# A hybrid decoder step on one core: the memory's statistics, the order of the key projections and the even mixer's PSUM tiles

## The chip, the cores and the metric

The kernel runs on one NeuronCore of a Trainium2 chip, as one launch. The metric is the device time of that launch in microseconds (us); a lower time is better. Five engines take part: TensorE (PE, matmuls; its weight loads are listed as PEld), VectorE (DVE), ScalarE (ACT), GpSimd (POOL) and SyncE (SP), which issues most of the DMAs. Each engine works through its own list of instructions in the order in which they were written, and waits where an operand or a buffer isn't ready.

## The reference

It is one inference step of a decoder with two layers, for 256 prompt tokens and 8 x 8 sample tokens that share all weights. The kernel handles them as 320 columns. All is float32, the model width is 2048.

```
layer i:  x += Mixer_i(rmsnorm(x))            # i = 0: even mixer, i = 1: odd mixer
          x += MemCrossAttn(rmsnorm(x), mem)
          x += SqReLU_MLP(rmsnorm(x))
even:     [silu(layernorm(dwconv(glu(h W)))), dilated attention(h W)] W_out
def mem_kv(mem, g_mem, wk, wv, kn):           # mem: 256 rows of 2048, the same in both layers
    m = rmsnorm(mem, g_mem)
    k = rmsnorm((m @ wk) as 4 heads of 128, kn)
    v = (m @ wv) as 4 heads of 128
```

The prompt's queries attend over these keys and values; the sample tokens attend over given caches. The keys and values of both layers are outputs too. The mean square of a memory row depends on the memory alone, so one value serves K and V of both layers, and since it scales a whole row, it can be applied to the projected row.

## The kernel before

**Weights.** All weight matrices are streamed in a fixed order as 800 "halves" of 128 x 1024 float32 (512 KB, tile `raw`, issued by SP, four buffers). Each half is split into two fp32r parts: ACT makes `whi` (L152), DVE makes the rest `wlo` (L153), three halves before PE uses them. An activation is split in the same way into `h` and `l`, and each product is three matmuls: whi by h, whi by l, wlo by h (L220 to L222). A half is 24 matmuls of 320 columns.

**Lanes.** Everything that isn't a product of the stream runs in Python generators ("lanes"). `pump()` and `mini()` advance each of them by a step after a half or half of one, and the instructions are emitted at that place. So the order on every engine is written out by the program; a scheduler doesn't change it. A `yield` in a lane moves what follows it to the next step.

**Around the change.** The stages are: the even mixer (input projection, convolution, attention), its output projection (even_out, eight residual steps p = 0 to 7), memory attention of layer 0 (K0, q, V0, K1, wo: K1 is the key projection of layer 1), FFN 0, the odd mixer, memory attention of layer 1 (q, V1, wo), FFN 1.

- `memkv(l, part)` makes a projection of the memory. Its `prep(k)` splits one of 16 blocks of 128 x 256: hi on ACT (L274), lo on DVE (L275), from a piece `z` of the memory (256 KB; 8 pieces). For K0 (`sums=True`), ACT also squares each piece (L303) and POOL adds the squares up (L304). `ahead(n)` prepares the first n blocks; in `body` five blocks are prepared before PE uses the first (L344 to L346 for keys, 256 columns; L352 to L354 for values, 512 columns).
- `statistics()` sums the squares over the partitions with a matmul by ones (L320) and makes the reciprocal root (`newton`) in `mrow` and `rcol`. It runs in the lane "fin" after K0, ahead of the keys' own norm: `finish()` squares the scaled keys and sums them by a matmul (L388, two instructions for each of two halves p).
- In even_out's residual step, DVE adds the product to `x` (L900), ACT makes the next activation's high parts and a square (L884, L889), DVE the low parts and the running sum of squares (L893, L896). K0's first pieces are loaded at p = 4, and its first three blocks prepared at p = 6 (L988 and after).
- After the last step, POOL sums the squares of `x` across the partitions (`across`, L253), and ACT and DVE make `rr`.
- In the even mixer, PSUM has, beside the two tiles of the main products, one tile of two banks (`pn`) and two single banks (`pa`). Scores (L779, L781), turned probabilities, weights per head (L706) and the convolution's layer norm take tiles from them; a new tile waits until the reader of the old one is done.

Of the kernel before, what the change touches and what calls it, by code (L numbers as in the profile page):

```python
# [20 lines left out]
P = 128  # L21
T = 320
# [86 lines left out]
def program(nc, tc, i, o):  # L109
# [12 lines left out]
    pn = es.enter_context(tc.tile_pool(name="pn", bufs=1, space=PSUM))  # L122
    pa = es.enter_context(tc.tile_pool(name="pa", bufs=2, space=PSUM))
# [157 lines left out]
    def memkv(l, part, new, sums=False, follow=None, deep=3):  # L281


        piece, hl, acc = {}, {}, []

        def load(q):
# [3 lines left out]
            elif follow:  # L290
                follow[0](q - 8)

        def prep(k):
# [22 lines left out]

        def statistics():
            V.tensor_add(out=acc[0][:, 0, :], in0=acc[0][:, 0, :], in1=acc[0][:, 1, :])
            ps = mk(pa, [P, 512], "a")
            mm(out=ps[:, :TP], lhsT=ones, rhs=acc[0][:, 0, :], start=True, stop=True)  # L320
            s, r = new("mrs", [P, TP], F32), new("mr", [P, TP], F32)
            newton(ps[:, :TP], D, s, r)
            V.tensor_mul(out=r, in0=r, in1=s)
            mrow.append(r)

            t = acc[0].rearrange("p a (b c) -> p (a b) c", c=P)[:, :2, :]
            V.tensor_mul(out=t, in0=r.rearrange("p (b c) -> p b c", c=P), in1=bc(ident, 2))
            V.tensor_reduce(out=rcol, in_=t, axis=AX.X, op=ALU.add)

        def body():  # L330
# [36 lines left out]
            if part == "K" and not sums:  # L367
# [7 lines left out]
            def finish():  # L375
                while l and (lanes.get("pr") or lanes.get("sa")):
                    yield
                if sums:
                    yield
                    statistics()  # L380
                    scaled()
                for p, z in enumerate(zs):
# [3 lines left out]
                    yield from pause(1 + l)  # L386
# [10 lines left out]
        return start, ahead, body, load  # L397
# [4 lines left out]
    with tc.tile_pool(name="even", bufs=1) as ep:  # L402
# [133 lines left out]
        def conv_ln():  # L536
            yield from pause(4)
            ps = mk(pn, [P, 2, 512], "n")
            for e in range(2):
                mm(out=ps[:, 0, :T], lhsT=ones, rhs=ysum[:, e, :], start=(e == 0), stop=(e == 1))  # L540
            mean = mk(ep, [P, T], "odd")
            nc.scalar.mul(out=mean, in_=ps[:, 0, :T], mul=1.0 / 1024)
# [10 lines left out]
            ps = mk(pn, [P, 2, 512], "n")  # L553
            for e in range(2):
                mm(out=ps[:, 0, :T], lhsT=ones, rhs=ysum[:, e, :], start=(e == 0), stop=(e == 1))
            s, r = mk(ep, [P, T], "cbuf", bufs=2), mk(ep, [P, T], "odd")
            newton(ps[:, 0, :T], 1024, s, r)
# [44 lines left out]
        def values(vs, pr, g):  # L602
# [6 lines left out]
            n = mk(pn, [P, 2, 512], "n")  # L609
            for e in range(4):  # L610
                nc.tensor.transpose(n[:, 0, e * P:e * P + P], vs[:, e // 2, (e % 2) * P:(e % 2) * P + P], ident)
            vt = mk(ep, [P, 4, P], f"vtok{g}")
            nc.scalar.copy(out=vt.rearrange("p a b -> p (a b)"), in_=n[:, 0, :])
            vtok[pr, g] = vt
            if g == 2:
                yield
                yield
                n = mk(pn, [P, 2, 512], "n")
                for s in range(4):
                    nc.tensor.transpose(n[:96, 0, s * P:s * P + P], vcat[pr][:, s, :], ident)  # L620
                vn = mk(ep, [P, 4, P], "vnew")
                nc.scalar.copy(out=vn[:96].rearrange("p a b -> p (a b)"), in_=n[:96, 0, :])
# [147 lines left out]
        def prompt(pr):  # L770
# [3 lines left out]
            for h in range(2):  # L774
                qk_ = [(qk[pr, 0, g][:, h, :], qk[pr, 1, g][:, h, :]) for g in range(3)]
                Sp = mk(ep, [P, 1152], "Sp")
                ps, n = mk(pa, [P, 512], "a"), mk(pn, [P, 2, 512], "n")
                for g, (q, k) in enumerate(qk_):
                    mm(out=ps[:, g * P:g * P + P], lhsT=q[:, :P], rhs=k[:, :P], start=True, stop=True)  # L779
                for g, (q, k) in enumerate(qk_):  # L780
                    mm(out=n[:, g // 2, g % 2 * TP:g % 2 * TP + TP], lhsT=q[:, P:TP], rhs=k[:, :TP], start=True, stop=True)  # L781
# [14 lines left out]
                ps, n = mk(pa, [P, 512], "a"), mk(pn, [P, 2, 512], "n")  # L796
                for g, dst in enumerate((ps, n[:, 0, :], n[:, 1, :])):
# [3 lines left out]
                nc.scalar.copy(out=pt[:, 0, :], in_=ps[:, :384])  # L801
                nc.scalar.copy(out=pt[:, 1:3, :], in_=n[:, :, :384])
# [68 lines left out]

    xp = es.enter_context(tc.tile_pool(name="xp", bufs=1))
# [63 lines left out]
    def memattn(l, before):  # L936

        with tc.tile_pool(name=f"mem{l}", bufs=1) as mp:
            KV = 3
            kvt = {}  # L940
            turn = {"first": itertools.cycle(("Xh6", "Xl6", "Xl7", "Xh0", "Xl0", "Xh1", "Xl1")), "mhl": itertools.cycle([f"Y{c}{n}" for n in range(4) for c in "hl"]), "mf": itertools.cycle(("Xl6", "Xl7")),
                    "mraw": itertools.cycle(("xacc", "xsq", "xsq"))}

            def room0(name, shape, dt):
                if name == "mhl":
                    return mk(base, shape, next(turn["first"]), dt, 1)
                if name in ("macc", "msq"):
                    return mk(base, shape, {"macc": "Xh7", "msq": "Xl5"}[name], dt, 1)
                if name == "mraw":
                    return mk(xp, shape, "z", dt, 2)  # L950
                if name in ("mk0", "mk1"):
                    return mkt[:, 2 * int(name[2]):2 * int(name[2]) + 2, :].rearrange("p a b -> p (a b)")
                return room(name, shape, dt)

            def room(name, shape, dt):
                if name in ("mf0", "mf1", "mf2"):
                    return mk(base, shape, next(turn["mf"]), dt, 1)
                if name == "mhl":
                    return mk(xp, shape, next(turn["mhl"]), dt, 1)
                if name in ("mv0", "mv1"):  # L960
                    return mvt[:, int(name[2]), :]
                if name == "mraw":
                    t = next(turn[name])
                    return mk(xp, shape, t, dt, {"xacc": 1, "xsq": 2}[t])
                if name in ("mrs", "mr"):
                    return mk(*((xp, [P, T], "rs") if name == "mrs" else (mp, shape, "mr")), dt)[:, :TP]
                return mk(xp, shape, "z", dt, 2)

            mstart, mahead, mbody, mload = memkv(1, "KV"[l], room)
            nstart, nahead, nbody, _ = memkv(0, "V", room, follow=(mload, mahead)) if l == 0 else (mstart, mahead, None, None)  # L970
# [71 lines left out]
            def prompt():  # L1042
# [39 lines left out]
                yield from pause(2 - l)  # L1082
                for p in range(2):
# [8 lines left out]
                    if l == 0:  # L1092
                        yield

            def sample():
                for p in range(2):
                    while p not in ready:
                        yield
                    yield from pause(5 - 3 * l * p)
# [21 lines left out]
                    while l and p and not have:  # L1121
# [19 lines left out]
            gemm(src, evac(0), after=lambda q: nstart() if q == 3 else None)  # L1141
            gemm(src, evac(1), after=lambda q: nahead(6) if q == 2 else None)
            if nbody:
                nbody()
                have.append(1)
            mbody()
# [367 lines left out]
```

## Time and profile before

| | us |
|---|---|
| median of 3 runs | 2978.48 (2975.43 to 2978.82) |
| the profiled execution | 2979.26 |
| its span, first to last instruction | 2977.5 |
| PE busy | 2936.9 (99%) |
| DVE busy | 1660.1 (56%) |
| ACT busy | 1195.6 (40%) |
| POOL busy | 133.8 (4%) |
| DMA, mean over the span | 170 GB/s |
| TensorE's mean granted clock | 0.995 |

The chain that ended last runs over PE for 95% of the span. An idle time of PE is therefore time of the kernel; an idle time of another engine matters where PE waits for it. All times in the rows are microseconds from the start of the span, unless a row says ns. The names of tiles are the program's, without buffer numbers.

### The profile page before, as it was taken

To read this page: it belongs to the slowest core of one execution; us is meant where nothing else is said; L and a number is where in the kernel's file an instruction comes from. 1 tells how busy PE (TensorE), PEld (TensorE's weight loads), DVE (VectorE), ACT (ScalarE), POOL (GpSimd) and SP (SyncE) were. 2 spreads that over 40 slices of the span, in tenths; PEclk is the share of its full clock that TensorE was granted. 3 is DMA by queue.
4 is the path that set the end of the run, shared out by engine and by line. 5 is a ranking of instruction groups with operands and counts; after the bars stand their busy time and mean duration, and the time that the engine had idled before them with its cause. 6 is when DMAs were issued, how large, how long until landed. Compare 5 with 4: busy or idle time off the path is not lost.

```text
span 2977.5 us, 49080 instructions
## 1 busy us (share of the span) xinstructions
PE 2936.9 (99%) x20828; PEld 2893.5 (97%) x20828; DVE 1660.1 (56%) x1903; ACT 1195.6 (40%) x1493; POOL 133.8 (4%) x115
## 2 busy tenths in 40 slices
PE   8999989899999999999999999999999999999999
PEld 8999989789999999999999999999999999999999
DVE  7887965577544544544545467557544544544543
ACT  6544454465333333333334344446332332332332
POOL 2210310200000000000000000000000000000000
PEclk9999999899999999999999999999999999999999
DMA  6774676464444444444444444555444444444443
GB/s 244 278 273 140 220 252 224 156 252 158 151 149 148 150 150 148 154 150 142 156 149 161 151 150 147 195 181 199 152 149 149 150 152 152 149 149 149 150 157 126
DMA packets 142253, 506.84 MB, mean 170 GB/s; under 512 B 16209, under 2 KB 18769, under 8 KB 139985
## 3 DMA queue, kind: packets, MB, share of 16 engines
q1 hardware_dynamic: 139536, 495.77, 47.5%
q0 software_dynamic: 2496, 7.92, 0.7%
q8 instruction: 163, 2.67, 0.4%
q14 instruction: 58, 0.47, 0.0%
HBM read 493.09 MB, written 10.54 MB: 169 GB/s over the span
## 4 chain that ended last, share of the span: by engine, by line
PE 95%; DVE 2%; ACT 1%; issue 1%; DMA 0%; POOL 0%; SPq 0%; DVEq 0%; POOLq 0%; ACTq 0%
PE g L220 30%; PE g L222 30%; PE g L221 29%; DVE wlo L153 1%; PE g L352 1%; PE g L354 0%; PE g L353 0%; PE a L689 0%; PE g L345 0%; PE a L718 0%; PE g L346 0%; PE g L344 0%; ACT whi L152 0%; DMA raw<-in_wall 0%; PE n L1297 0%
## 5 line engine op out<-in xcount | busy, mean ns | idle before, releaser
L153 DVE TENSOR_TENSOR wlo<-raw,whi 128x1024 fp32r<-128x1024 f32 x800 | 994.8, 1252 | 916.0 <-ACT whi L152 898.8
L152 ACT CAST whi<-raw 128x1024 fp32r<-128x1024 f32 x800 | 835.9, 1049 | 1119.9 <-PE g L221 1069.4
L220 PE MATMUL g<-Xh,whi 128*128 128x320 f32 x3424 | 1061.5, 310 | 8.7 <-ACT whi L152 8.4
L222 PE MATMUL g<-Xh,wlo 128*128 128x320 f32 x3424 | 1055.5, 308 | 0.4 <-DVE wlo L153 0.4
L221 PE MATMUL g<-Xl,whi 128*128 128x320 f32 x3424 | 1055.6, 308 | 0.0
L220 PE MATMUL g<-Yh,whi 128*128 128x320 f32 x2688 | 834.0, 310 | 2.2 <-DVE x L900 2.2
L222 PE MATMUL g<-Yh,wlo 128*128 128x320 f32 x2688 | 831.3, 309 | 0.0
L221 PE MATMUL g<-Yl,whi 128*128 128x320 f32 x2688 | 831.2, 309 | 0.0
L220 PEld LDWEIGHTS g<-Xh,whi 128*128 128x128 f32 x3424 | 643.8, 188 | 14.7 <-ACT whi L152 9.0
L221 PEld LDWEIGHTS g<-Xl,whi 128*128 128x128 f32 x3424 | 643.8, 188 | 0.5 <-issue 0.2
L222 PEld LDWEIGHTS g<-Xh,wlo 128*128 128x128 f32 x3424 | 643.5, 188 | 0.8 <-DVE wlo L153 0.8
L220 PEld LDWEIGHTS g<-Yh,whi 128*128 128x128 f32 x2688 | 505.3, 188 | 4.0 <-issue 3.5
L221 PEld LDWEIGHTS g<-Yl,whi 128*128 128x128 f32 x2688 | 505.2, 188 | 0.7 <-issue 0.5
L222 PEld LDWEIGHTS g<-Yh,wlo 128*128 128x128 f32 x2688 | 505.2, 188 | 0.0
L270 ACT CAST Xh<-z 128x640 fp32r<-128x640 f32 x72 | 52.3, 727 | 300.8 <-DVE z L1188 273.7
L1187 DVE TENSOR_TENSOR z<-g,rr 128x640 f32<-128x640 f32 x64 | 52.8, 825 | 82.5 <-PE g L222 82.5
L271 DVE TENSOR_TENSOR Xl<-z,Xh 128x640 fp32r<-128x640 f32 x72 | 59.5, 826 | 57.1 <-ACT Xh L270 57.1
L1203 DVE TENSOR_TENSOR x<-x,g 128x640 f32<-128x640 f32 x48 | 39.4, 821 | 64.9 <-PE g L222 64.9
L524 DVE SCALAR_TENSOR_TENSOR y<-cbuf,cst,y 128x320 f32<-128x320 f32 x120 | 68.5, 570 | 2.7 <-ACT y L522 2.7
L900 DVE TENSOR_TENSOR x<-x,g 128x640 f32<-128x640 f32 x48 | 39.4, 821 | 53.8 <-PE g L222 52.8
L253 POOL PARTITION_ALL_REDUCE xacc<-xacc x7 | 19.6, 2796 | 1102.7 <-DVE xacc L921 956.7
L524 DVE SCALAR_TENSOR_TENSOR odd<-cbuf,cst,odd 128x320 f32<-128x320 f32 x112 | 61.4, 548 | 0.0
(337 smaller groups left out, 1477.5 us busy)
## 6 DMA issues: line engine op xcount, KB each, us to landing
raw<-in_wall SPq DMA_DIRECT2D x800, 512.0 KB, 3.3
kv<-in_kv SPq DMA_DIRECT2D x72, 512.0 KB, 6.5
kv<-in_memc SPq DMA_DIRECT2D x16, 1024.0 KB, 6.9
xsq<-in_mem SPq DMA_DIRECT2D x15, 256.0 KB, 4.2
x<-in_x SPq DMA_DIRECT2D x8, 320.0 KB, 5.2
out_y<-x SPq DMA_DIRECT2D x8, 320.0 KB, 2.3
xacc<-in_mem SPq DMA_DIRECT2D x9, 256.0 KB, 3.6
z<-in_mem SPq DMA_DIRECT2D x8, 256.0 KB, 2.8
```

What stands on the lines that cost most here:

```text
L152: nc.scalar.copy(out=hi, in_=src)
L153: V.tensor_sub(out=lo, in0=src, in1=hi.bitcast(F32))
L220: mm(out=out, lhsT=w1, rhs=ah, start=(k == 0), stop=False)
L221: mm(out=out, lhsT=w1, rhs=al, start=False, stop=False)
L222: mm(out=out, lhsT=w2, rhs=ah, start=False, stop=(k == nk - 1))
L270: nc.scalar.copy(out=hi, in_=src)
L271: V.tensor_sub(out=lo, in0=src, in1=hi.bitcast(F32))
L352: mm(out=out, lhsT=m1, rhs=w1, start=(k == 0), stop=False)
L524: V.scalar_tensor_tensor(out=out, in0=buf[:, :, j:j + 8], scalar=w, in1=out, op0=ALU.mult, op1=ALU.add)
L900: V.tensor_add(out=x[p], in0=x[p], in1=ps[:, :, :T])
L1187: V.tensor_mul(out=z, in0=ps[:, :, :T], in1=bc(r.r, 2))
L1203: V.tensor_add(out=x[p], in0=x[p], in1=ps[:, :, :T])
```

## The change

- **Statistics.** They leave `memkv` and become a generator `memstat` in a lane "stat", which runs beside even_out. It loads the eight pieces of the memory once more, squares each in its own buffer on ACT, adds on DVE (not POOL), and ends with the matmul by ones and `newton`.
- **Order of the stream in layer 0.** It was K0, q, V0, K1; now it is K0, K1, q, V0. K1's body follows K0's directly and has blocks of its own (eight tiles; K0 has seven). K0 starts K1's loads and first blocks.
- **K0's start.** Its first two loads are issued at p = 6 (before at p = 4), and its first three blocks are prepared at p = 7 (before at p = 6). Both keys are scaled by `mrow` at the end of their body.
- **Lanes of layer 0.** `finish` has one `yield` and waits for nothing else. The prompt and sample lanes have the pauses that layer 1 had.
- **PSUM of the even mixer.** A pool `pe` of four single banks takes the place of `pn` and `pa`, which are opened after the even mixer. The scores' mask is added in three pieces (384, 512 and 256 columns; before 384 and 768), and the turned probabilities are copied in three pieces of 384 columns (before 384 and 768).

```
             memkv(0, "K")
+            memkv(1, "K")
         pairs("wq_mem", l, list(range(16)), 2)
-        if l == 0:
-            memkv(0, "V")
-        memkv(1, "KV"[l])
+        memkv(l, "V")
...
+    def memstat(new):
+        piece = {}
+        def load(q):
+            if q < 8:
+                piece[q] = new("mraw", [P, 2, TP], F32)
+                nc.sync.dma_start(out=piece[q], in_=i["mem"][q])
+        load(0)
+        load(1)
+        acc = new("macc", [P, 2, TP], F32)
+        yield
+        for q in range(8):
+            yield
+            sq = piece[q] if q else acc
+            act(out=sq, in_=piece[q], func=AF.Square)
+            if q:
+                V.tensor_add(out=acc, in0=acc, in1=sq)
+            load(q + 2)
+        V.tensor_add(out=acc[:, 0, :], in0=acc[:, 0, :], in1=acc[:, 1, :])
+        yield
+        ps = mk(pa, [P, 512], "a")
+        mm(out=ps[:, :TP], lhsT=ones, rhs=acc[:, 0, :], start=True, stop=True)
...
             if e == 1:
-                if sums and q == 0:
-                    acc.append(new("macc", [P, 2, TP], F32))
-                    act(out=acc[0], in_=piece[q], func=AF.Square)
-                elif sums:
-                    sq = new("msq", [P, 2, TP], F32)
-                    act(out=sq, in_=piece[q], func=AF.Square)
-                    nc.gpsimd.tensor_add(out=acc[0], in0=acc[0], in1=sq)
                 load(q + deep)
...
-            if part == "K" and not sums:
+            if part == "K":
                 scaled()
...
-                while l and (lanes.get("pr") or lanes.get("sa")):
-                    yield
-                if sums:
-                    yield
-                    statistics()
-                    scaled()
...
-                    yield from pause(1 + l)
+                    yield
                     ps = mk(pa, [P, 512], "a")
                     mm(out=ps, lhsT=ones, rhs=sq, start=True, stop=True)
...
-    with tc.tile_pool(name="even", bufs=1) as ep:
+    with tc.tile_pool(name="even", bufs=1) as ep, tc.tile_pool(name="pe", bufs=4, space=PSUM) as pa:
...
-                ps, n = mk(pa, [P, 512], "a"), mk(pn, [P, 2, 512], "n")
+                ps, n = mk(pa, [P, 512], "a"), [mk(pa, [P, 512], "a") for _ in range(2)]
...
-                V.tensor_add(out=Sp[:, 384:], in0=n.rearrange("p a b -> p (a b)")[:, :768], in1=mb[:, SW + 384:])
+                V.tensor_add(out=Sp[:, 384:896], in0=n[0], in1=mb[:, SW + 384:SW + 896])
+                V.tensor_add(out=Sp[:, 896:], in0=n[1][:, :TP], in1=mb[:, SW + 896:])
...
-                start0, ahead0, body0, _ = memkv(0, "K", room0, sums=True, deep=2)
-                src = before(lambda p: {4: start0, 6: lambda: ahead0(3)}.get(p, lambda: None)())
+                start1, ahead1, body1 = memkv(1, "K", room("K1"))
+                start0, ahead0, body0 = memkv(0, "K", room("K0"), follow=(start1, ahead1), deep=2)
+                lane("stat", memstat(room("K0")))
+                src = before(lambda p: {6: start0, 7: lambda: ahead0(3)}.get(p, lambda: None)())
                 r = rlane()
                 body0()
+                body1()
```

In the rows below a name is a tile with the numbers of its buffer; a line number is that of its own kernel, and the added lines shift the later kernel's: L153 is L150 there, L275 is L272, L893 and L896 are L900 and L903, L900 is L907, L253 is L250, L304 has no counterpart, L388 is L392.

DVE at the end of even_out and the start of K0, before. `x_698` is the residual of p = 7, the `L275` rows are the low parts of K0's blocks:

```order
558 L275 SCALAR_TENSOR_TENSOR Xl_785_5723<-z_5516,gain_72,Xl_785_5723 128x256
559 L275 SCALAR_TENSOR_TENSOR Xl_788_5730<-z_5518,gain_72,Xl_788_5730 128x256
560 L153 TENSOR_TENSOR wlo_5737<-raw_5622,whi_5736 128x1024
561 L153 TENSOR_TENSOR wlo_5771<-raw_5656,whi_5770 128x1024
562 L153 TENSOR_TENSOR wlo_5801<-raw_5686,whi_5800 128x1024
563 L900 TENSOR_TENSOR x_698_5117<-x_698_5117,g_5733 128x640
564 L893 SCALAR_TENSOR_TENSOR Yl_715_5145<-x_697_5116,gain_72,Yh_707_5137 128x320 x2
565 L896 TENSOR_TENSOR xacc_5186<-xacc_5186,xsq_5742 128x640
566 L893 SCALAR_TENSOR_TENSOR Yl_716_5146<-x_698_5117,gain_72,Yh_708_5138 128x320 x2
567 L896 TENSOR_TENSOR xacc_5186<-xacc_5186,xsq_5834 128x640
568 L275 SCALAR_TENSOR_TENSOR Xh_802_5840<-z_5518,gain_72,Xh_802_5840 128x256
569 L275 SCALAR_TENSOR_TENSOR Xl_805_5848<-z_5728,gain_72,Xl_805_5848 128x256
```

The same place now:

```order
574 L150 TENSOR_TENSOR wlo_5788<-raw_5682,whi_5787 128x1024
575 L150 TENSOR_TENSOR wlo_5822<-raw_5716,whi_5821 128x1024
576 L150 TENSOR_TENSOR wlo_5852<-raw_5746,whi_5851 128x1024
577 L907 TENSOR_TENSOR x_706_5137<-x_706_5137,g_5784 128x640
578 L900 SCALAR_TENSOR_TENSOR Yl_723_5165<-x_705_5136,gain_66,Yh_715_5157 128x320 x2
579 L903 TENSOR_TENSOR xacc_5211<-xacc_5211,xsq_5793 128x640
580 L900 SCALAR_TENSOR_TENSOR Yl_724_5166<-x_706_5137,gain_66,Yh_716_5158 128x320 x2
581 L903 TENSOR_TENSOR xacc_5211<-xacc_5211,xsq_5885 128x640
582 L272 SCALAR_TENSOR_TENSOR Xh_816_5890<-z_5780,gain_66,Xh_816_5890 128x256
583 L272 SCALAR_TENSOR_TENSOR Xl_817_5893<-z_5780,gain_66,Xl_817_5893 128x256
584 L272 SCALAR_TENSOR_TENSOR Xl_819_5898<-z_5782,gain_66,Xl_819_5898 128x256
585 L272 SCALAR_TENSOR_TENSOR Xh_821_5902<-z_5782,gain_66,Xh_821_5902 128x256
```
Before, the low parts of blocks 0 to 2 stood ahead of three weight splits and the residual of p = 7. Now all low parts, from block 0 on, stand behind that residual.

POOL from the end of the even mixer, before. A row `ISA` without operands stands wherever it goes from its other work to the adds (L304), from these to the sum across partitions (L253), and back:

```order
67 L304 ISA
68 L304 TENSOR_TENSOR Xh_786_5726<-Xh_786_5726,Xl_803_5843 128x512
69 L304 TENSOR_TENSOR Xh_786_5726<-Xh_786_5726,Xl_810_5872 128x512
70 L253 ISA
71 L253 ISA xacc_5186<-xacc_5186 128x320
72 L304 ISA
73 L304 TENSOR_TENSOR Xh_786_5726<-Xh_786_5726,Xl_817_5915 128x512
```
The same place now:

```order
66 L611 COPY vcat_4445<-ev_4918 128x4x32
67 L250 ISA xacc_5211<-xacc_5211 128x320
68 L398 DMA out_memk<-mk_5149 128x512 x2
69 L1013 MEMSET Xl_927_6541 128x640
```
The adds and the operandless rows beside them are gone; the sum across partitions stays, and K1's and K0's outputs follow it.

PE in wo of layer 0, before: the second of K1's two fin products (a row is one product by ones) stands between main products of wo:

```order
4094 L221 MATMUL g_7466<-Xl_860_6170,whi_7343 128x320
4095 L222 MATMUL g_7466<-Xh_858_6168,wlo_7344 128x320
4096 L388 MATMUL a_7505<-Xl_1095_7425,ones_74 128x512
4097 L220 MATMUL g_7516<-Xh_857_6167,whi_7378 128x320
4098 L221 MATMUL g_7516<-Xl_859_6169,whi_7378 128x320
```
Now the same fin product stands between main products of q (`Yh`, `Yl` are q's input):

```order
3708 L218 MATMUL g_6551<-Yl_722_5164,whi_6507 128x320
3709 L219 MATMUL g_6551<-Yh_714_5156,wlo_6508 128x320
3710 L392 MATMUL a_6657<-Xl_945_6625,ones_68 128x512
3711 L217 MATMUL g_6551<-Yh_715_5157,whi_6554 128x320
3712 L218 MATMUL g_6551<-Yl_723_5165,whi_6554 128x320
```
It moved from behind V0 to ahead of it.

## Rows read from the trace of the kernel before

**Rows 1.** Waits of PE: line, releaser: us in total, times, longest us
```profile
...
PE g L344 <- ACT Xh L274: 11.9, 1, 11.9
...
PE a L706 <- DVE Sp L783: 4.6, 1, 4.6
PE g L220 <- DVE x L900: 2.2, 1, 2.2
...
PE a L779 <- ACT ppad L708: 1.9, 1, 1.9
...
PE a L750 <- ACT ppad L708: 0.8, 1, 0.8
...
PE n L611 <- ACT pt L802: 0.6, 1, 0.6
...
```

**Rows 2.** Windows by stage (the third line names the columns)
```profile
core 0: us, PE busy (x) PEld busy (x) DVE busy (x) ACT busy (x) POOL busy (x), PEclk, DMA share, GB/s
545.20:586.70 41.50, 26.81 (x193) 25.63 (x193) 24.92 (x32) 21.04 (x34) 15.83 (x11) 0.79 0.35 121
586.70:717.00 130.30, 126.35 (x938) 113.82 (x936) 94.46 (x149) 83.22 (x145) 7.22 (x10) 1.00 0.60 214
717.00:831.30 114.30, 114.26 (x769) 114.29 (x770) 64.78 (x68) 41.96 (x47) 2.96 (x1) 0.99 0.44 153
1973.30:2071.80 98.50, 98.47 (x736) 89.05 (x735) 69.58 (x111) 64.58 (x114) 7.87 (x7) 1.00 0.57 205
2071.80:2184.50 112.70, 112.70 (x771) 112.70 (x770) 63.01 (x66) 42.27 (x47) 4.19 (x1) 1.00 0.45 154
475.00:545.20 70.20, 70.20 (x481) 70.20 (x480) 40.34 (x48) 33.89 (x46) 0.00 (x0) 1.00 0.67 244
```

**Rows 3.** Windows where the granted clock was at half; same columns
```profile
404.30:411.10 6.80, 5.04 (x42) 4.67 (x42) 6.58 (x11) 5.29 (x10) 0.00 (x0) 0.50 1.03 356
438.40:441.80 3.40, 3.40 (x11) 2.86 (x11) 1.12 (x3) 0.64 (x1) 0.00 (x0) 0.50 1.00 394
564.70:581.80 17.10, 6.66 (x29) 6.37 (x30) 7.42 (x10) 8.33 (x14) 6.55 (x4) 0.50 0.29 97
718.30:721.70 3.40, 3.40 (x15) 3.40 (x14) 3.40 (x6) 1.52 (x4) 0.00 (x0) 0.50 0.44 165
```

**Rows 4.** Timeline of POOL, first half of K0: start, us, what [idle before]
```profile
...
560.56 2.17 POOL L253 PARTITION_ALL_REDUCE xacc<-xacc  x1 [6.94 <-DMA raw<-in_wall]
569.49 1.25 POOL L304 TENSOR_TENSOR Xh<-Xh,Xl 128x512 f32<-128x512 f32 x1 [6.76 <-issue]
...
```

**Rows 5.** Timeline of ACT in the same stretch
```profile
...
570.78 0.63 ACT L303 ACTIVATE Xl<-z 128x512 f32<-128x512 f32 x1 [11.32 <-POOL Xh L304]
...
```

**Rows 6.** Timeline of DVE at the start of K0
```profile
...
545.38 0.82 DVE L900 TENSOR_TENSOR x<-x,g 128x640 f32<-128x640 f32 x1 [1.32 <-PE g L222]
...
549.45 1.50 DVE L275 SCALAR_TENSOR_TENSOR Xh<-z,gain,Xh 128x256 fp32r<-128x256 f32 x1
550.86 0.47 DVE L275 SCALAR_TENSOR_TENSOR Xl<-z,gain,Xl 128x256 fp32r<-128x256 f32 x1
...
```

**Rows 7.** Timeline of ACT at the start of K0
```profile
...
547.79 0.50 ACT L274 ACTIVATE Xh<-z,gain 128x256 fp32r<-128x256 f32 x1
...
```

**Rows 8.** Timeline of PE in K1: two matmuls, twelve apart
```profile
...
655.99 0.28 PE L344 MATMUL g<-Yl,whi 128*128 128x256 f32 x1
...
657.43 0.28 PE L344 MATMUL g<-Yh,whi 128*128 128x256 f32 x1
...
```

**Rows 9.** Timeline of PE: one fin product (two instructions)
```profile
...
706.37 1.02 PE L388 MATMUL a<-Xl,ones 128*128 128x512 f32 x2
...
```

**Rows 10.** The page's part 5: the split of one half on DVE
```profile
...
L153 DVE TENSOR_TENSOR wlo<-raw,whi 128x1024 fp32r<-128x1024 f32 x800 | 994.8, 1252 | 916.0 <-ACT whi L152 898.8
...
```

**Rows 11.** Timeline of DVE at the end of wo
```profile
...
714.34 0.69 DVE L393 TENSOR_TENSOR z<-z,Xl 128x512 f32<-128x512 f32 x1
...
716.08 0.81 DVE L900 TENSOR_TENSOR x<-x,g 128x640 f32<-128x640 f32 x1
...
```

More of the change, by code (lines that the diff above doesn't have):

```diff
@@ L289, in load, with memkv @@
                 nc.sync.dma_start(out=piece[q], in_=i["mem"][q])
-            elif follow:
-                follow[0](q - 8)
+        load(0)
[13 more added lines that the diff above has]
+        mm(out=ps[:, :TP], lhsT=ones, rhs=acc[:, 0, :], start=True, stop=True)
+        s, r = new("mrs", [P, TP], F32), new("mr", [P, TP], F32)
+        newton(ps[:, :TP], D, s, r)
+        V.tensor_mul(out=r, in0=r, in1=s)
+        mrow.append(r)
+        t = acc.rearrange("p a (b c) -> p (a b) c", c=P)[:, :2, :]
+        V.tensor_mul(out=t, in0=r.rearrange("p (b c) -> p b c", c=P), in1=bc(ident, 2))
+        V.tensor_reduce(out=rcol, in_=t, axis=AX.X, op=ALU.add)
+    def memkv(l, part, new, follow=None, deep=3):
+        piece, hl = {}, {}
+        def load(q):
+            if q < 8:
+                piece[q] = new("mraw", [P, 2, TP], F32)
+                nc.sync.dma_start(out=piece[q], in_=i["mem"][q])
+            elif follow and q == 8:
+                follow[0]()
         def prep(k):
@@ L315, in ahead @@
                 follow[1](n - 16)
[L317 to L328, printed above, removed]
         def body():
@@ L396, in body @@
                 lane("fin", finish())
-        return start, ahead, body, load
+        return start, ahead, body
     X = slot(base, "X", 8)
     mb = mk(base, [P, MW], "mask", BF16)
-    with tc.tile_pool(name="even", bufs=1) as ep:
+    with tc.tile_pool(name="even", bufs=1) as ep, tc.tile_pool(name="pe", bufs=4, space=PSUM) as pa:
         KVR = 4
@@ L795, in prompt @@
                 pt = mk(ep, [P, 3, 384], "pt", bufs=2)
-                ps, n = mk(pa, [P, 512], "a"), mk(pn, [P, 2, 512], "n")
-                for g, dst in enumerate((ps, n[:, 0, :], n[:, 1, :])):
+                turned = [mk(pa, [P, 512], "a") for _ in range(3)]
+                for g, dst in enumerate(turned):
                     nc.tensor.transpose(dst[:, :P], Sp[:, g * P:g * P + P], ident)
@@ L800, in prompt @@
                         nc.tensor.transpose(dst[:, P + c * P:2 * P + c * P], Sp[:, 384 + g * TP + c * P:384 + g * TP + c * P + P], ident)
-                nc.scalar.copy(out=pt[:, 0, :], in_=ps[:, :384])
-                nc.scalar.copy(out=pt[:, 1:3, :], in_=n[:, :, :384])
+                for g, dst in enumerate(turned):
+                    nc.scalar.copy(out=pt[:, g, :], in_=dst[:, :384])
                 pts.append(pt)
@@ L869, in program @@
         drain()
+    pn = es.enter_context(tc.tile_pool(name="pn", bufs=1, space=PSUM))
+    pa = es.enter_context(tc.tile_pool(name="pa", bufs=2, space=PSUM))
     xp = es.enter_context(tc.tile_pool(name="xp", bufs=1))
@@ L955, in room @@
[L955 to L967, printed above, removed]
@@ L969, in memattn @@
-            mstart, mahead, mbody, mload = memkv(1, "KV"[l], room)
-            nstart, nahead, nbody, _ = memkv(0, "V", room, follow=(mload, mahead)) if l == 0 else (mstart, mahead, None, None)
+            turn = {"K0": itertools.cycle(("Xh6", "Xl6", "Xl7", "Xh0", "Xl0", "Xh1", "Xl1")),
+                    "K1": itertools.cycle([f"X{c}{n}" for n in (2, 3, 4, 5) for c in "hl"]),
+                    "V": itertools.cycle([f"Y{c}{n}" for n in range(4) for c in "hl"]),
+                    "mf": itertools.cycle(("Xl6", "Xl7")), "mraw": itertools.cycle(("xacc", "xsq", "xsq"))}
@@ new lines, in room, with new @@
+            def room(which):
+                def new(name, shape, dt):
+                    if name in ("mf0", "mf1", "mf2"):
+                        return mk(base, shape, next(turn["mf"]), dt, 1)
+                    if name == "mhl":
+                        return mk(xp if which == "V" else base, shape, next(turn[which]), dt, 1)
+                    if name in ("mv0", "mv1"):
+                        return mvt[:, int(name[2]), :]
+                    if name in ("mk0", "mk1"):
+                        return mkt[:, 2 * int(name[2]):2 * int(name[2]) + 2, :].rearrange("p a b -> p (a b)")
+                    if name == "macc":
+                        return mk(base, shape, "Xh7", dt, 1)
+                    if name == "mraw" and which != "K0":
+                        t = next(turn[name])
+                        return mk(xp, shape, t, dt, {"xacc": 1, "xsq": 2}[t])
+                    if name in ("mrs", "mr"):
+                        return mk(*((xp, [P, T], "rs") if name == "mrs" else (mp, shape, "mr")), dt)[:, :TP]
+                    return mk(xp, shape, "z", dt, 2)
+                return new
@@ L971, in memattn @@
+            vstart, vahead, vbody = memkv(l, "V", room("V"))
             mkt, mvt, have = mk(mp, [P, 4, TP], "mk"), mk(mp, [P, 2, 512], "mv"), []
@@ L1081, in prompt @@
                     yield
-                yield from pause(2 - l)
+                yield
                 for p in range(2):
@@ L1120, in sample @@
                     yield from pause(3)
-                    while l and p and not have:
+                    while p and not have:
                         yield
@@ L1140, in memattn @@
             lane("pr", prompt())
[L1141 to L1146, printed above, removed]
+            gemm(src, evac(0), after=lambda q: vstart() if q == 3 else None)
+            gemm(src, evac(1), after=lambda q: vahead(6) if q == 2 else None)
+            vbody()
             have.append(1)
```

46 lines of the change are left out of this document (15 added, 31 removed).

## The prediction

> **What bounds the kernel now.** I read the chain that ended last and the busy times first: PE is busy for 99% of the span, so only time that PE loses, or work that it is spared, can move the end. The change spares PE nothing: the same matmuls are issued. So the second view is the waits of PE, and the reader is to see in it how few there are: one of 11.9 us in K0, one of 4.6 and several below 2 in the even mixer, one of 2.2 at the end of wo in layer 0 [rows 1]. The third view is the windows by stage, because a stage also loses what its clock loses. Here memory attention of layer 1 serves as a model: q, V1 and wo, 98.5 us, with PE busy for 98.47 of them [rows 2]. The fourth is the granted clock. It stood at 0.50 (the lower of 1.2 and 2.4 GHz) in four stretches that bear on the change, and each followed an idle time of PE: 4.6, 1.9, 11.9 and 2.2 us [rows 1, 3]. The 1.3 us wait at K0's fourth block was followed by none, as no such stretch lies before 564.7.
>
> **K0 itself.** K0 takes 41.5 us [rows 2]. Its 192 matmuls of 256 columns start 12 in 1.44 us where nothing is late [rows 8], so 192 x 0.120 = 23.0 us; 18.5 us are lost. The cause is on POOL: 6.94 us idle before the sum across partitions, 2.17 us of that sum, and 6.76 us idle before its next add, with no other wait named for that [rows 4]. ACT's next square waits 11.32 us for POOL's add [rows 5], and the high parts and weight casts of K0 are behind that square on ACT. With the adds on DVE beside even_out and the squares gone from K0, nothing in K0 waits for POOL: in the new order POOL has only the sum across partitions there. This sum feeds `rr`, which q's output needs; K0 and K1 now lie between, 46 us of matmuls against 2.17 us of POOL. So the 18.5 us go, as far as nothing else is late.
>
> Something is. Before, the first three blocks were ready when even_out ended; now their low parts stand behind the residual of p = 7 on DVE. That residual begins 545.38, when the last product is there, and the first low part behind it began at 549.45 [rows 6]. The high part on ACT began at 547.79 [rows 7], so it isn't last. The low part took 1.50 us there with POOL's adds beside it, and the next one 0.47 [rows 6]; I take 0.5. PE's first K0 matmul by a low part then starts near 549.95, and only one matmul, by the first high part, can come earlier: about 4.7 us of idle time from 545.2. I add a clock loss as after the idle time most like it, 4.6 us: PE was busy for 5.04 us at half speed [rows 3], which costs 2.5 us. The bounds are 0 (as after the 1.3 us wait) and 3.3 (6.66 us of busy time at half after the 11.9 us wait [rows 3]). K0 becomes 23.0 + 4.7 + 2.5 = 30.2, a gain of 11.3 us.
>
> By the Trainium skill ("TensorE: Matmul & The Clock Gate", "HAM oscillation — how this bites in real kernels") the penalty is the whole throttled time times one half. That would be 6.8 / 2 = 3.4 us after such a wait. The trace agrees where PE is busy throughout: 3.4 us at half clock at the start of FFN 0, so 1.7, against 114.3 - 112.7 = 1.6 us lost [rows 2, 3]; of the 6.8 us 1.8 were idle. By the page's sum the time would be 0.9 us later.
>
> **K1, q, V0, wo.** These took 130.3 us [rows 2]. After the change PE's list for q, V0 and wo is that of layer 1, 98.5 us. Ahead of it stands K1 (23.0), and into K1 and q come the four fin products of K0 and K1, 1.02 us each [rows 9], 4.1 in all. The sum is 125.6, 4.7 less. Of this about 0.5 isn't gained: the statistics' product (half the columns of a fin product) moves beside even_out. 4.2 us remain. They include the 2.2 us wait at the end of wo, where DVE had K1's fin work (L393 and its like) ahead of the last residual [rows 1, 11]; that work now lies beside q.
>
> **FFN 0.** With that wait the half clock behind it goes: 114.3 - 112.7 = 1.6 us [rows 2].
>
> **Even mixer.** Of the waits there, L750 (0.8) and L611 (0.6) wait for a copy on ACT that holds the tile, and so does L779 (1.9) [rows 1]; with four single banks another is free. Of L779's I leave 0.3, since one of its three tiles still follows such a copy. That is 0.8 + 0.6 + 1.6 = 3.0 us, and the 3.4 us of busy time at half clock behind L779 [rows 3] give 1.7. I leave the 4.6 us at L706: the weights' tile takes the bank of the score tile that DVE reads before, and that read stands behind the convolution's layer norm on DVE, as before. So 4.7 us; the bounds are 0 and 4.7 + 7.1 (the rival below). The additional instructions (a third DVE add, a third ACT copy per head) lie where these engines have room.
>
> **Beside even_out.** Here DVE is busy for 40.3 and ACT for 33.9 of 70.2 us, DMA at 0.67 [rows 2]. Added are eight squares (0.63 each, as L303 [rows 5]), seven adds (0.69 each, as L393 for that shape [rows 11]) and 2 MB of loads on SP. The engines come to 45 and 39 us; the loads, at 244 GB/s over 70.2 us, raise the share from 0.67 to 0.75. PE doesn't wait there now, and its weights are split three halves ahead (a half is 70.2 / 20 = 3.5 us). I take 0, with an upper end below.
>
> **Pace of K0 and K1.** For a half of 2.88 us DVE needs 1.25 for the weights [rows 10] and 2 x 0.47 [rows 6], 2.2. In K1 it also has K0's scaling (2 x 0.7) and fin work (two times four instructions of at most 0.7, 5.6). So 8 x 2.2 + 7.0 = 24.6 against K1's 23.0 + 2.0 of PE, with blocks prepared during K0 in reserve. That is close; I allow 0.5 us of waits.
>
> **Sum.** 11.3 + 4.2 + 1.6 + 4.7 - 0.5 = 21.3 us from the profiled execution, 2979.26: 2958.0. That execution is 0.8 us above the median of the runs, 2978.48. I predict 2957.
>
> **Rivals.**
> - *The 4.6 us at L706 go as well.* The new tiles take the four banks in turn, and a free one may be there when the weights are turned. Then 4.6 and the 2.5 behind it are gained: 2957 - 7 = 2950. Against it: the other banks are taken at that place, by the scores among others. The Trainium skill ("Perfetto Trace Analysis", "Matmuls") lets independent groups rotate through banks so that the eviction of one overlaps the next; by that rule the trace should show the wait gone. Chance 0.12.
> - *The even mixer's PSUM gives nothing.* All tiles come from one pool now, so the layer norm and the values' transposes compete with scores for it; a wait removed at L779 comes back at another tile. 2957 + 4.7 = 2962. For it: the engines that free the banks are no faster. Chance 0.15.
> - *The keys run at the pace of their splits.* K0 starts with no block ready, its pieces come through two buffers, and K1 has DVE at 24.6 of 25.0 us. If the idle time at K0's start is 7 instead of 4.7 and K1's DVE loses 15% (3.7 us) to waits of its own, each with some more half clock (2 us), the time is 2957 + 2.3 + 3.7 + 2 = 2965. Against it: in layer 1 the same splits with as much beside them let PE run for 98.47 of 98.5 us. Chance 0.16.
> - *Slower: the memory's loads beside even_out hold the weights up.* SP issues them between those of `raw` and behind 2.6 MB of `x`, and ACT's square, which waits for a piece, stands ahead of a weight cast. The cover is three halves, 10.5 us. If a piece lands later than that, PE stands still; one half's time (3.5 us) for each of eight pieces is 28 us, so 2985. From about six such pieces on the gain of 21.3 us is used up. Against it: two buffers let each load start a step ahead, and the DMA share is 0.67. Chance 0.03.
>
> **How the numbers follow.** The forecast has 0.51, and 0.03 is left for what I haven't seen. The forecast's own range, from the clock at K0 and half of the small waits, is 2953 to 2961. The range reaches down over the first rival to 2949, and up over the second and third to 2967. A measurement of this kernel can tell about 0.2%, 6 us, from no change; faster means below 2972.5. All cases but the last, and a part of the unseen, are: 0.92. The third rival with a larger loss, or half the last, ends within: 0.05. Slower 0.03.
>
> **What would show it.** Right: K0's stage near 30 us with one PE wait of 4 to 5 us at its start, which ends at a low part on DVE (the L272 row), half clock behind it for some 5 us, no POOL wait; q to wo at 98 to 100 us and FFN 0's first 768 matmuls at 112.7; no wait of PE at the scores in the even mixer over 0.5 us, but L706's still there. Wrong: waits of PE in even_out, a K1 over 27 us, or a K0 that still waits for ACT in its middle.

## The result and the profile after

| | before | changed |
|---|---|---|
| median, us | 2978.65 | 2955.46 |
| range of 4 runs, us | 2975.43 to 2979.9 | 2955.29 to 2955.51 |
| profiled execution, us | 2979.26 | 2955.49 |
| its span, us | 2977.5 | 2953.4 |

The ratio is 0.9924, with a 95% interval from 0.9906 to 0.9941: 23 us less. The forecast was 2957 us, and 2955.46 were measured.

The stages first, in the windows that answer to those of [rows 2]: from the first matmul to the end of even_out (536.8 us before: 8.4 to 545.2), K0, then K1 to wo, FFN 0, and q to wo of layer 1. The columns are the stretch, its length, the busy time of PE, PEld, DVE, ACT and POOL with their instructions, PE's granted clock, the DMA share and GB/s.

```profile
...
9.10:540.60 531.50, 525.32 (x4232) 505.76 (x4232) 418.10 (x591) 281.90 (x405) 77.13 (x59) 0.99 0.65 236
540.60:570.10 29.50, 25.45 (x195) 24.97 (x194) 22.34 (x36) 17.84 (x32) 3.29 (x1) 0.88 0.59 198
570.10:694.60 124.50, 124.47 (x937) 113.15 (x936) 92.21 (x145) 81.82 (x142) 8.96 (x13) 1.00 0.62 222
694.60:807.20 112.60, 112.60 (x770) 112.60 (x769) 63.08 (x66) 42.22 (x47) 4.19 (x1) 1.00 0.45 153
1949.30:2047.80 98.50, 98.47 (x736) 89.06 (x736) 69.62 (x111) 64.64 (x114) 7.88 (x7) 1.00 0.57 205
...
```

K0 went from 41.5 to 29.5 us, K1 to wo from 130.3 to 124.5, FFN 0 from 114.3 to 112.6, and the stretch up to even_out's end from 536.8 to 531.5. The gains are 12.0, 5.8, 1.7 and 5.3; 0.7 is lost at the very start, where the first weights came that much later (9.1 against 8.4 us; in the profiled runs below this wait is 7.8 to 8.7 us, so it is not the change's). That is the 24.1 us between the spans. The stage of layer 1 takes 98.5 us in both.

PE's waits (line, releaser: us in total, times, longest), to be held against [rows 1]:

```profile
...
PE g L217 <- ACT whi L149: 9.1, 1, 9.1
PE a L710 <- DVE Sp L787: 4.3, 1, 4.3
PE g L354 <- ACT Xh L271: 3.0, 1, 3.0
PE a L785 <- ACT ppad L712: 1.1, 1, 1.1
PE g L355 <- DVE Xh L272: 1.1, 1, 1.1
...
```

The 11.9 us wait in K0, the waits at the sample scores and value transposes, and the 2.2 us wait at the end of wo are gone. L710 (L706 before) still waits for DVE's add. Two new rows, L354 and L355, are K0's first two products; here they are on PE's timeline, and then the instructions that released them on ACT and DVE (start, us, what, in brackets the idle time before):

```profile
...
540.48 0.31 PE L219 MATMUL g<-Xh,wlo 128*128 128x320 f32 x1
543.77 0.58 PE L354 MATMUL g<-Xh,whi 128*128 128x256 f32 x1 [2.99 <-ACT Xh L271]
545.41 0.58 PE L355 MATMUL g<-Xh,whi 128*128 128x256 f32 x1 [1.06 <-DVE Xh L272]
...
```
```profile
...
541.68 1.01 ACT L891 ACTIVATE Yh<-x,gain 128x320 fp32r<-128x320 f32 x2 [3.43 <-DVE x L907]
...
543.22 0.49 ACT L271 ACTIVATE Xh<-z,gain 128x256 fp32r<-128x256 f32 x1
...
```
```profile
...
540.82 0.82 DVE L907 TENSOR_TENSOR x<-x,g 128x640 f32<-128x640 f32 x1 [1.32 <-PE g L219]
...
544.15 0.82 DVE L903 TENSOR_TENSOR xacc<-xacc,xsq 128x640 f32<-128x640 f32 x1
544.88 0.48 DVE L272 SCALAR_TENSOR_TENSOR Xh<-z,gain,Xh 128x256 fp32r<-128x256 f32 x1
...
```

The high part of block 0 follows the residual's work on ACT, and its low part the residual's on DVE, as the order showed. The low part takes 0.48 us; with POOL's adds beside it the first one took 1.50 [rows 6]. Behind the 4.05 us of idle time the clock is at half:

```profile
...
543.20:550.00 6.80, 5.17 (x22) 4.87 (x23) 3.92 (x10) 3.28 (x8) 0.00 (x0) 0.50 0.47 149
...
```

Beside the outputs of the keys, only the sum across partitions is left on POOL in K0 and K1. It starts when DVE has added the halves (L928), with no idle time behind a switch as in [rows 4]:

```profile
...
552.19 3.29 POOL L250 PARTITION_ALL_REDUCE xacc<-xacc  x1 [101.42 <-DVE xacc L928]
```

### The profile page after: what moved, and what is told of

It is laid out like the page before. It is cut to its first block, busy times and chain, and to the rows that moved or that the text cites. A ratio compares the mean times of both kernels' runs of the same rounds, so it can differ in the third digit from the quotient of the medians.

```text
span 2953.4 us, 49092 instructions
## 1 busy us (share of the span) xinstructions
PE 2929.6 (99%) x20828; PEld 2888.6 (98%) x20828; DVE 1658.0 (56%) x1914; ACT 1195.4 (40%) x1497; POOL 124.1 (4%) x108
## 4 chain that ended last, share of the span: by engine, by line
PE 97%; DVE 1%; DMA 1%; ACT 1%; issue 0%; SPq 0%; DVEq 0%; ACTq 0%
PE g L217 30%; PE g L219 30%; PE g L218 30%; PE g L355 1%; PE g L354 1%; PE g L356 1%; PE g L362 1%; PE g L364 1%; PE g L363 0%; PE a L693 0%; DMA kv<-in_kv 0%; PE a L722 0%; DVE wlo L150 0%; PE n L1299 0%; PE a L1133 0%
## 5 line engine op out<-in xcount | busy, mean ns | idle before, releaser
L150 DVE TENSOR_TENSOR wlo<-raw,whi 128x1024 fp32r<-128x1024 f32 x800 | 993.6, 1250 | 904.6 <-ACT whi L149 883.5
L250 POOL PARTITION_ALL_REDUCE xacc<-xacc x7 | 21.9, 3134 | 1225.2 <-DVE xacc L928 1086.2
L907 DVE TENSOR_TENSOR x<-x,g 128x640 f32<-128x640 f32 x48 | 39.3, 819 | 51.8 <-PE g L219 50.8
```

Of the source, the lines that this page charges most:

```text
L150: V.tensor_sub(out=lo, in0=src, in1=hi.bitcast(F32))
L907: V.tensor_add(out=x[p], in0=x[p], in1=ps[:, :, :T])
```

## The experiments

Each was timed in five rounds beside the kernel before, whose medians in these rounds were 2978 to 2979 us. The ranges are those of a kernel's runs; the numbers e1 to e10 serve to name them.

**e1: K0's blocks early again.**

```
-                src = before(lambda p: {6: start0, 7: lambda: ahead0(3)}.get(p, lambda: None)())
+                src = before(lambda p: {5: start0, 6: lambda: ahead0(3)}.get(p, lambda: None)())
```

> The changed kernel, but K0's first two loads at p = 5 and its first three blocks at p = 6, so ahead of the last residual again. If K0's start waits because its first blocks stand behind that residual, the two waits there (2.99 and 1.06 us) shrink to at most 1.3 us in all, the granted clock stays at 1.00, and with the 5.17 us of busy time at half speed gone (2.6 us) the time is 2955.5 - 2.8 - 2.6 = 2950, down to 2949. Rival: the wait only moves, to the fourth block, behind the same residual; the clock falls there too, and the time is 2953 to 2956.

Measured: 2950.40 us (2949.32 to 2952.02), ratio 0.9905 [0.9892, 0.9919], 5 us under the changed kernel. PE's waits, with the same line numbers as above; L355 now is all of K0:

```profile
...
PE a L710 <- DVE Sp L787: 4.1, 1, 4.1
PE a L785 <- ACT ppad L712: 1.1, 1, 1.1
...
PE g L355 <- DVE Xh L272: 0.3, 1, 0.3
PE g L355 <- DVE Xl L272: 0.3, 1, 0.3
```

Both waits at K0's start are gone. At the fourth block, where the rival saw them go, 0.3 us is left (the L355 row with `Xh`, at 543.98). K0's window:

```profile
...
539.20:563.80 24.60, 23.95 (x195) 23.02 (x194) 20.04 (x32) 16.09 (x29) 2.15 (x1) 1.00 0.62 219
...
```

It is 24.6 us now, with the clock at 1.00 throughout. So the later preparation of K0's blocks is a cost inside the change, and can be had back.

**e2: the even mixer's PSUM as before**, all else as changed.

```
-    with tc.tile_pool(name="even", bufs=1) as ep, tc.tile_pool(name="pe", bufs=4, space=PSUM) as pa:
+    with tc.tile_pool(name="even", bufs=1) as ep:
...
-                turned = [mk(pa, [P, 512], "a") for _ in range(3)]
-                for g, dst in enumerate(turned):
+                ps, n = mk(pa, [P, 512], "a"), mk(pn, [P, 2, 512], "n")
+                for g, dst in enumerate((ps, n[:, 0, :], n[:, 1, :])):
```

> The changed kernel with the even mixer's PSUM as before (one tile of two banks, two single banks, the adds and copies in two pieces). If the four single banks took PE's waits away, they come back: about 0.8 us at the sample scores, 0.6 at the value transposes, 1.9 at the prompt scores with 3.4 us at half clock behind it; 2955.5 + 5 = 2960 to 2961. Rival: the even mixer's gain came from something else (the place of the statistics, which of several tiles waits is chance), and the time stays within 1.5 us of 2955.5.

Measured: 2960.52 us (2958.68 to 2961.03), ratio 0.9938 [0.9925, 0.9950]. The waits of before are back with their sizes, and so is a stretch at half clock behind the prompt scores. Line numbers are those of this run's kernel: L785 is the prompt scores' first product (L783 in the changed kernel, L779 in the one before), L756 the sample scores, L617 the value transposes.

```profile
...
PE a L785 <- ACT ppad L714: 1.9, 1, 1.9
...
PE a L756 <- ACT ppad L714: 0.8, 1, 0.8
PE n L617 <- ACT pt L808: 0.6, 1, 0.6
PE a L771 <- ACT ppad L714: 0.5, 1, 0.5
...
```
```profile
...
438.30:441.60 3.30, 3.30 (x11) 2.76 (x10) 1.13 (x3) 0.48 (x1) 0.00 (x0) 0.50 0.97 386
...
```

The four banks are worth 5.1 us.

**e3: POOL's adds of before on DVE**, all else as before.

```
-                    nc.gpsimd.tensor_add(out=acc[0], in0=acc[0], in1=sq)
+                    V.tensor_add(out=acc[0], in0=acc[0], in1=sq)
```

> The kernel before with one edit: K0's seven adds of squares are on DVE, not POOL; order, statistics and tiles as before. If POOL's switch between the adds and the sum across partitions was K0's stall, the 11.9 us wait and the half clock around it go, K0 takes 25 to 28 us and the time is 2963 to 2966. Rival: the memory's pieces (two buffers) or the statistics hold K0 up, K0 stays above 37 us, and the time is within 4 us of 2978.5.

Measured: 2963.01 us (2959.34 to 2964.42), ratio 0.9945 [0.9933, 0.9958]. One word gives 16 us. Between the profiled spans it is 17.4: 14.8 in K0, 1.6 in FFN 0, where the clock did not fall in this execution, and most of the rest at the first weights. The windows are K0, then q to wo, then FFN 0; the row below them is POOL's sum across partitions, whose idle time before it is that since POOL's last work in the even mixer:

```profile
...
544.30:571.00 26.70, 24.05 (x194) 22.97 (x193) 24.10 (x38) 20.94 (x34) 3.87 (x4) 1.00 0.50 176
571.00:701.20 130.20, 126.25 (x938) 113.91 (x936) 94.89 (x150) 83.41 (x145) 7.04 (x10) 1.00 0.63 217
701.20:813.90 112.70, 112.67 (x768) 112.70 (x769) 63.93 (x68) 41.85 (x47) 4.12 (x1) 1.00 0.49 155
...
```
```profile
...
552.96 2.15 POOL L253 PARTITION_ALL_REDUCE xacc<-xacc  x1 [98.82 <-DMA raw<-in_wall]
...
```

K0 took 41.5 us before and takes 26.7 here, and q to wo 130.2, as before. So POOL's adds, with the switches around them, held K0 up. This run doesn't part the adds from the switches, but the trace of the kernel before does. It names the switch, an instruction MODIFY_POOL_CONFIG on POOL's sequencer (line, instruction, count, shortest/median/longest ns, start of the first and the last):

```profile
...
L253 POOLq MODIFY_POOL_CONFIG  x2: 8/8/8, 553.8 to 553.9; - x2
...
```
```profile
...
L304 POOLq MODIFY_POOL_CONFIG  x2: 98/98/98, 562.7 to 562.7; - x2
...
```

One pair stands between the last add (551.40, 2.23 us long) and the sum at 560.56, the other between that sum and the next add at 569.49; the idle times of 6.94 and 6.76 us in [rows 4] lie there, while an add takes 1.3 to 2.2 us. In the changed kernel and in this run the only pair lies near 38 us, before any of this. The changed kernel's K0 (29.5) is longer than this one, e1's (24.6) is shorter: with the statistics out of K0 the stage gains another 2 us, and the later blocks cost 5.

**e4: K1 behind V0**, all else as changed.

```
-            memkv(1, "K")
         pairs("wq_mem", l, list(range(16)), 2)
         memkv(l, "V")
+        if l == 0:
+            memkv(1, "K")
...
                 body0()
-                body1()
...
             vbody()
             have.append(1)
+            if l == 0:
+                body1()
```

> The changed kernel with K1 where it was, behind V0, with V0's block tiles; statistics beside even_out, lanes and PSUM as changed. If it is K1's place that cleared the end of wo, a wait of PE of about 2 us for the last residual returns there, FFN 0 starts with 3.4 us at half clock, and small waits in wo; 2955.5 + 5 to 7.5 = 2960 to 2963. Rival: the single yield and the layer-1 pauses in the lanes cleared it, and the time stays at 2955 to 2957.

Measured: 2959.51 us (2958.54 to 2960.50), ratio 0.9935 [0.9922, 0.9949]; 4.0 us above the changed kernel. The windows are q to wo, with K1 in it, and FFN 0; the rows below them are PE's waits in the late part of the stage (a fin product, a residual, wo's first product):

```profile
...
570.10:698.70 128.60, 125.72 (x936) 113.70 (x936) 91.64 (x142) 82.82 (x143) 7.04 (x10) 1.00 0.62 216
698.70:811.30 112.60, 112.60 (x769) 112.60 (x769) 63.79 (x68) 41.78 (x47) 4.12 (x1) 1.00 0.48 155
...
```
```profile
...
PE a L393 <- ACT Xl L390: 1.3, 1, 1.3
...
PE g L218 <- DVE x L908: 0.8, 1, 0.8
PE g L1168 <- DVE z L375: 0.6, 1, 0.6
...
```

The loss is all in q to wo, 128.6 us against 124.5 for K1 to wo in the changed kernel; FFN 0 takes 112.6 us in both. The 2.2 us wait ahead of FFN 0 [rows 1], which the theory wanted back, did not return. The 0.8 us for a residual lies at 691.55, two products ahead of FFN 0's first at 698.67, behind the second fin's work on DVE, and no stretch at half clock follows. So both theories have a part: K1's place is worth 4 us, in small waits inside wo, and the rest of the 7.5 us of K1 to FFN 0, the wait ahead of FFN 0 among it, went with the other edits of the change in the lanes and the statistics. No run parts these two.

**e8: the seven adds on POOL beside even_out**, all else as changed.

> The changed kernel (not e1), but the seven adds of squares beside even_out are on POOL instead of DVE. Theory: what cost K0 its time was the place of the adds, in K0 behind a switch of POOL and ahead of ACT's square, so beside even_out POOL may add at no cost: 2955.5 within 1.5 us, and the sum across partitions may wait for a switch of some 7 us without PE noticing. Rival: POOL's adds slow DVE's work beside them, and a switch holds up the square that follows: PE waits in even_out or K0, 2958 or more.

The edit is `nc.gpsimd.tensor_add` for `V.tensor_add` in `memstat`. Measured: 2954.30 us (2953.71 to 2954.95), ratio 0.9920 [0.9905, 0.9935], no slower than with DVE. POOL's timeline, the last adds and the sum; then POOL's switch, and an instruction pair on DVE beside the add at 498.30:

```profile
...
498.30 1.29 POOL L296 TENSOR_TENSOR Xh<-Xh,z 128x512 f32<-128x512 f32 x1 [1.68 <-ACT z L294]
501.30 4.36 POOL L296 TENSOR_TENSOR Xh<-Xh,z 128x512 f32<-128x512 f32 x2 [1.72 <-ACT z L294]
551.41 2.29 POOL L250 PARTITION_ALL_REDUCE xacc<-xacc  x1 [45.75 <-DVE xacc L928]
...
```

```profile
...
L250 POOLq MODIFY_POOL_CONFIG  x2: 4/4/4, 505.9 to 505.9; - x2
...
```
```profile
...
498.36 2.05 DVE L900 SCALAR_TENSOR_TENSOR Yl<-x,gain,Yh 128x320 fp32r<-128x320 f32 x2
...
```

So POOL may do these adds where nobody waits for them. The switch is still there, right behind the last add, but the sum comes 45 us later and finds it done. The rival's first half is true as well: the pair on DVE takes 2.05 us beside the add, and 1.01 at this place in the changed kernel. PE does not wait for it; its waits from 470 us to the sum are those at K0's start.

**e5 to e10: the wait at the turned weights.** Three attempts on what is left, all on top of e1. The first (e5) issues the weights later.

```
                 if c % 2:
-                    weights(c + 1)
                     kv_to(min(36 * pr + 23 + 2 * c, 36 * pr + 35))
-                    yield from pause(AHEAD)
+                    yield from pause(2)
+                    weights(c + 1)
+                    yield from pause(AHEAD - 2)
```

> The kernel of e1 with one more edit: in the attention lanes the turned weights (the product that waited 4.1 us for a bank, L710) are issued two steps later, and the pause behind them is two steps shorter. Theory: PE's list then has main products (two steps, some 3.5 us) ahead of the waiting product, so the wait falls from 4.1 to 0.5 to 1 us and the half clock behind it goes (3.4 us in e1, 1.7 lost): 2950.4 - 3.3 - 1.7 = 2945 to 2946. Rival: the copies behind the weights on ACT come later in the same measure, and PE waits at the sample products (L722) or the scores instead: 2949 to 2953.

Measured: 2952.13 us (2951.06 to 2953.38), ratio 0.9913 [0.9898, 0.9927]. The time is the rival's, but the waits are not where it put them: they moved to the value transposes (L615) and the turned probabilities (L804), behind the same two engines:

```profile
...
PE a L804 <- ACT ppad L712: 3.5, 1, 3.5
PE a L615 <- DVE Sp L788: 2.6, 1, 2.6
...
```

The second (e6, e7) moved the scores of the first head pair, by one step and by two:

```
-            yield from pause((16, 4)[pr])
+            yield from pause((15, 4)[pr])
```

> The kernel of e1 with the first prompt scores one step earlier (pause of 15, not 16). Theory: DVE's adds of the mask, which free the bank, then stand ahead of part of the convolution's layer norm; the wait of 4.1 us falls to 2 or less, with or without half clock behind it: 2946 to 2949. Rival: the adds stay behind the same chain, and the time stays at 2950.

> The kernel of e1 with the first prompt scores two steps earlier (14, not 16). Theory: all three adds stand ahead of the layer norm's second half on DVE, the wait at the turned weights goes (under 0.5 us) with the half clock behind it: 2950.4 - 4.1 - 1.7 = 2944.6, 2944 to 2947. Rival: the scores themselves now wait, for a bank that the layer norm's sum or the weights hold, by 1 to 3 us: 2948 to 2952.

Measured: 2950.87 (2950.01 to 2951.76) and 2950.86 us (2949.97 to 2951.69): no change. I had misread which scores DVE was late with. The scores ahead of the wait stood on PE at 394.63 us in e1 and at 394.55 in e7; they are those of the second pair, whose pause is the other number.

The third (e9, e10) moved these, by one step (`(16, 3)`) and by two (`(16, 2)`):

> The kernel of e1 with the prompt scores of the second head pair one step earlier (pause of 3, not 4); e6 and e7 had moved those of the first pair. DVE's adds of the mask now stand ahead of a weight split, one evacuation and four instructions of the layer norm (5.3 us in e1). Theory: the wait of 4.1 us for their bank falls under 0.5 us, and the half clock behind it (3.4 us) goes: 2950.4 - 3.8 - 1.7 = 2945, 2944 to 2947. Rival: the weight split or the layer norm, now behind the adds, come late and PE waits for these instead: 2948 to 2951.

> As e9, with the second pair's scores two steps earlier (pause of 2). Theory: DVE's list at the adds is that of e9, so the time is the same within 1.5 us, 2944 to 2947. Rival: two steps earlier the scores' tiles wait for a bank that the layer norm's sum or the turned weights hold, by 1 to 3 us: 2947 to 2951.

Measured: 2947.54 (2946.51 to 2948.33), ratio 0.9896 [0.9879, 0.9912], and 2950.24 us (2945.80 to 2951.26), ratio 0.9902 [0.9887, 0.9917]. PE's waits, of the first and then of the second:

```profile
...
PE a L559 <- DVE ysum L554: 2.0, 1, 2.0
PE a L783 <- DVE qk L597: 1.0, 1, 1.0
...
```
```profile
...
PE a L783 <- DVE qk L597: 3.0, 1, 3.0
PE a L615 <- DVE Sp L787: 1.2, 1, 1.2
...
```

The 4.1 us at L710 went, and in both profiled executions no stretch at half clock is left in the even mixer; but in e9 2.0 us came back at the layer norm's sum (L559), whose operand DVE now makes later, and 1.0 at the scores, which now wait for their normed keys. About half of the 5.5 us hoped for is kept. Two steps earlier, the scores wait 3.0 us for these keys; so it was the operand and not, as I had written, a bank. The step of one is the best version I have: 31 us under the kernel before, 8 under the changed one.

## Why the prediction was right

- **K0** was to take 30.2 us: 23.0 of matmuls, 4.7 of idle time, 2.5 for the clock. It took 29.5, with 4.05 us of idle time that ended at the low part on DVE, and 5.17 us of busy time at half clock (2.6 us). By the Trainium skill ("TensorE: Matmul & The Clock Gate", "HAM oscillation — how this bites in real kernels") the loss is estimated as half of the whole 6.8 us, 3.4. The trace does not bear this out here: 29.5 - 23.0 - 4.05 leaves 2.4, so the row that counts PE's busy time alone was the better measure. The idle time splits in two, since the first product needs the high part alone. e1 shows the wait and its cause, e3 that POOL was the old one, and the trace that POOL's idle times around its switches were.
- **K1 to wo** was to take 125.6 us and took 124.5; **FFN 0** 112.7 and took 112.6. That the list of layer 1 would run as in layer 1 held. The reason given for the end of wo was too strong: e4 gives K1's place 4.0 of the 7.5 us, and with K1 back behind V0 the wait ahead of FFN 0 and its half clock stayed away. So the sizes were right, and that K1's place cleared this wait isn't shown. (It was for the last residual but one: in the kernel before, the last follows on DVE at 719.61.) FFN 0's 1.6 us had some luck in it: in e3 the wait was there and the clock did not fall. The fin products were taken too dear: four cost 124.5 - 98.5 - 23.0 = 3.0 us, not 4.1.
- **The even mixer** was to give 4.7 us and gave 5.3, with the statistics' product that moved in already counted; e2 puts the PSUM part at 5.1. L785 waits 1.1 us where I left 0.3, so the sign of no wait over 0.5 us at the scores was missed; and q to wo took 100.2 us (594.4 to 694.6), where 98 to 100 was said. L710 stayed, as its bank's reader stood in the same place on DVE. The rule that products should rotate through banks (the Trainium skill, "Perfetto Trace Analysis", "Matmuls") held for the waits that went; at L710 four banks did not help, and e9 shows that the reader's place on its engine did.
- **Beside even_out** nothing was lost: PE has no wait there. **The allowance** of 0.5 us for the pace of the keys wasn't needed; PE is busy for 124.47 of 124.5 us.
- **The rivals.** The two on the fast and slow side of the PSUM part fell by the rows of L710 and by e2. The keys' pace fell by the last point, though its first half, a late start of K0, was in the forecast. The loads beside even_out never held PE up.

The terms were too small by 0.7 (K0), 1.1 (K1 to wo), 0.1 (FFN 0) and 1.1 us (up to the end of even_out: 5.3 against 4.7 - 0.5), and the 0.5 went unused: 3.5 in all. The late first weights took 0.7 back, so 21.3 + 2.8 = 24.1 between the spans. What the prediction had not seen is how the gain is made up: 16 us are to be had by the engine of one add alone (e3; 14.8 of them are K0's), and the change's own start of K0 gives 5 away (e1).

## What to carry to other kernels

Where an engine alternates between kinds of work that it must switch between (here a MODIFY_POOL_CONFIG with some 7 us of idle time each way), look for long idle times before both and price them at whoever waits in order behind that engine; changing the engine of a cheap add may be worth more than moving the work. When a step is moved past another, list what is queued ahead of its first product on every engine: here the blocks had lost their lead to one residual. And before moving an instruction away from a wait, name which instance of it waits.

## What the runs showed of the hardware

The same idle time of PE is not always followed by the lower clock. In the kernel before, 2.23 us ahead of FFN 0 was followed by 3.4 us at half [rows 3]; in e3 the same 2.23 us was not, and the window of FFN 0 above has a clock of 1.00. The first product of FFN 0, before and in e3:

```profile
...
717.04 0.38 PE L220 MATMUL g<-Yh,whi 128*128 128x320 f32 x1 [2.23 <-DVE x L900]
...
```
```profile
...
701.23 0.38 PE L220 MATMUL g<-Yh,whi 128*128 128x320 f32 x1 [2.23 <-DVE x L900]
...
```

The wait at L710 was followed by 6.8 us at half in the changed kernel and by 3.4 in e1, though it was 4.3 and 4.1 us. In e4 (L711 there) and e8 it was 4.57 us in both, followed by 3.4 us at half in e4 and by 6.8 in e8. The rows are, in this order, those of the changed kernel, e1, e4 and e8:

```profile
...
403.20:410.10 6.90, 4.69 (x21) 4.32 (x21) 6.74 (x12) 5.09 (x10) 0.27 (x1) 0.51 1.01 369
...
```
```profile
...
404.60:408.00 3.40, 3.40 (x14) 3.40 (x15) 3.40 (x6) 3.12 (x7) 0.00 (x0) 0.50 0.97 360
...
```
```profile
...
406.50:409.90 3.40, 3.40 (x16) 3.36 (x14) 3.40 (x6) 3.35 (x8) 0.00 (x0) 0.50 1.01 412
...
```
```profile
...
403.00:409.80 6.80, 5.22 (x43) 4.79 (x43) 6.63 (x12) 5.46 (x10) 0.00 (x0) 0.51 0.96 353
...
```

In e10, 3.0 us of idle time were followed by no drop in the profiled execution:

```profile
...
390.00:410.00 20.00, 17.05 (x187) 15.97 (x186) 17.65 (x30) 13.70 (x25) 3.34 (x3) 1.00 0.58 213
...
```

That execution took 2945.80 us, and the other three 2949.98 to 2951.26; the mean granted clock on record is 1.000 for it and 0.999 for each of the other three, which points to the clock. That it made the whole difference isn't shown, since they have no trace. For a forecast it means that idle times of 2 to 4.6 us came with a price from nothing to some 2.6 us, by an estimate of half the busy time at half clock, and that the length alone did not tell which.
